# Ten HBM tiles for first weight sums, and normalisation of q, k and spatial v in four parts

## The chip, the cores and the metric

One core of a Trainium2 chip runs the whole layer in one launch. The metric is the device time of one execution in microseconds. Five engines work side by side, each through its own queue of instructions: TensorE (PE; PEld are its weight loads), VectorE (DVE), ScalarE (ACT), GpSimd (POOL) and SyncE (SP), which here only issues DMA transfers. An engine waits for another through semaphores.

## What is computed

The reference is one decoder layer on 256 tokens of width 2048 in float32. An RMS norm of x is followed by one wide projection into nine parts: q, k, v and z_a for attention, u_b, v_b and z_b for spatial gating, and two gates g_a and g_b.

```python
h = rms_norm(x, norm_g)
q, k, v, z_a, u_b, v_b, z_b, g_a, g_b = jnp.split(h @ w_in, cuts, axis=-1)
q = rms_norm(q.reshape(B, S, 8, 128), q_norm_g)
k = rms_norm(k.reshape(B, S, 8, 128), k_norm_g)
y_a = (moba_attention(q, k, v) * jax.nn.silu(z_a)) @ w_proj_a
sgu = spatial_gating(gelu(u_b), gelu(v_b), sgu_norm_g, w_s, b_s)
y_b = (sgu * jax.nn.silu(z_b)) @ w_proj_b
return x + (sigmoid(g_a) * y_a + sigmoid(g_b) * y_b) @ w_out
```

With 256 tokens the attention is causal inside one block. spatial_gating normalises v_b per group of 128 columns (an RMS norm with a gain), mixes positions with a causal 128x128 matrix per group, and multiplies by u_b. So q, k and v_b are each normalised per head or group: a sum of squares over 128 columns, the inverse root, and a scaling.

## The kernel before, in words

**Work and its tiles.** Weights stream from HBM in 120 granules of 128 x 2048 floats (1 MB), each laid out by the host as four 128 x 512 blocks. The list `G` of `schedule()` has the order: 8 granules each for q (0 to 7), k (8 to 15), v (16 to 23), za (24 to 31), vb (32 to 39), ub (40 to 47) and zb (48 to 55); then four times 8 granules of a gate quad (the gates' columns) and 4 of a projection (56 to 103); then two out quads (104 to 119).

**Precision.** Every float32 product is made of three matmuls: a weight block is split into a high part `wh`, rounded to the type float32r, and a rest `wl`, and so is x; TensorE adds high times high, low times high and high times low (`three`, line 318, whose matmul is line 323). `split` (line 152) makes the parts: a cast on ScalarE (line 149 or 171) and a subtraction on VectorE (line 150 or 176).

**Sum granules.** Some granules of each quad after q are multiplied by a scheme with seven block products in place of eight (`strassen(i)` says which; `seven`, line 341). They also need three sums of weight blocks, `t` (VectorE, lines 172 to 174), split in turn into `th` (ScalarE, line 175) and `tl` (VectorE, line 177). Five of the eight granules of k, v, vb and zb are of this kind, four of za and ub, five of the first gate quad, six of the other three. There is one buffer for `t`, three each for `wh`, `wl` and `th`, two for `tl`, and four for `raw`, the loaded weights.

**The first weight sum, made in HBM.** The first of these sums (block 12 plus block 11) isn't made by an engine: `pre_copy` (line 127) has SyncE copy block 12 into a tile of the HBM ring, `pre_sum` (line 132) has GpSimd start a DMA that adds block 11 to it, and `load` (line 136) later loads that tile as the first block of `raw`, followed by the remaining 768 KB. The ring has six tiles (line 113). In iteration i of the main loop the load of granule i + 3 is issued, then the copy for i + 8 and the accumulation for i + 6, then the split of i + 2, and then granule i's matmuls.

```python
            load(i + 3)
        if i >= 1:
            pre_copy(i + 8)
            pre_sum(i + 6)
        split(i + 2, 2 if i < 2 else 1)
```

**Work between the granules.** The dictionary `later` says what is called behind the matmuls of a granule. `sums` (line 394) makes 16 sums of squares on ScalarE (line 401), four for each of the four 128 x 512 tiles of q, k or v_b, and per tile the inverse root: a small VectorE operation into `ms` (line 268), a power on GpSimd into `rs` (line 269) and, for k, a VectorE multiplication (line 406). `norm_qk` (line 409) and `norm_v` (line 417) scale with 16 ScalarE operations (lines 415 and 423); `norm_v` also multiplies by the gain on VectorE. For q the sums are called behind granule 9 and the scaling behind 11; for k behind 17 and 19; for v_b behind 42 and 44. Their consumers are the transposes `turn_qk` behind granules 16 (q) and 24 (k) and `mix` behind 48. `softmax` has two calls behind granule 26, and its results are transposed behind 32.

**What sets the order.** SyncE and GpSimd execute in the order in which the program is written, in the whole kernel (line 109). ScalarE and VectorE do so only for the first eight granules (line 658). From granule 8 on, their order and TensorE's come from a planner that runs when the program is built: it prefers instructions that stand earlier in the program, but lets a later one go first when it thinks that the earlier one isn't ready. Once planned, each engine's order is fixed.

Of the kernel before, what the change touches and what calls it, by code (L numbers as in the profile page):

```python
# [12 lines left out]
F32 = mybir.dt.float32  # L13
# [3 lines left out]
AF = mybir.ActivationFunctionType  # L17
ALU = mybir.AluOpType
AX = mybir.AxisListType

P = 128
# [8 lines left out]
B = 512  # L30
# [41 lines left out]
def hybrid_layer_kernel(  # L72
# [9 lines left out]
    nc = tc.nc  # L82
# [7 lines left out]
    small = ctx.enter_context(tc.tile_pool(name="small", bufs=4))  # L90
    psum = ctx.enter_context(tc.tile_pool(name="psum", bufs=1, space=bass.MemoryType.PSUM))
    dram = ctx.enter_context(tc.tile_pool(name="dram", bufs=1, space=bass.MemoryType.DRAM))
# [4 lines left out]
    def u(name, dtype=F32):  # L97
        return unit.tile([P, B], dtype, tag="u", name=name)
# [11 lines left out]

    raw, wh, wl, th, tl = {}, {}, {}, {}, {}
    pre = {}
    ring = [dram.tile([P, B], F32, tag=f"ring{n}", name=f"ring{n}") for n in range(6)]

    def strassen(i):
        if i >= NG or G[i][0] != "quad" or G[i][1] == G[0][1]:
# [10 lines left out]
    def pre_copy(i):  # L127
        if i < NG and strassen(i):
            pre[i] = ring[len(pre) % len(ring)]
            nc.sync.dma_start(pre[i], w[i, :, 0:B])  # L130

    def pre_sum(i):
        if i in pre:
            nc.gpsimd.dma_start(pre[i], w[i, :, B:2 * B], accum_op=ALU.add)  # L134
# [44 lines left out]
    X = {}  # L179

    def heads(ap):
        return ap.rearrange("p (h d) -> p h d", d=P)
# [65 lines left out]
    gain = const.tile([P, P], F32, name="gain")  # L248
# [17 lines left out]
    def rsqrt(dst, src, n, count):  # L266
        ms = small.tile([P, 8], F32, tag="ms", name="ms")
        nc.vector.tensor_scalar(ms[:, :n], src, 1.0 / count, EPS, op0=ALU.mult, op1=ALU.add)
        nc.gpsimd.tensor_tensor(dst, ms[:, :n], mhalf[:, :n], op=ALU.pow)
# [121 lines left out]
        return [[c11, c12], [h, c22]]  # L391


    def sums(C, name):
        for m in range(2):
            for c in range(2):
                ss = small.tile([P, 4], F32, tag="ss", bufs=8, name="ss")
                junk = u("junk")
                scale = rstd[:, m:m + 1] if name == "k" else 1.0
                for h in range(4):  # L400
                    nc.scalar.activation(junk[:, h * P:(h + 1) * P], C[m][c][:, h * P:(h + 1) * P], AF.Square,
                                         scale=scale, accum_out=ss[:, h:h + 1])
                rs = small.tile([P, 4], F32, tag="rs", bufs=8, name="rs")
                rsqrt(rs, ss, 4, P)
                if name == "k":
                    nc.vector.tensor_scalar(rs, rs, scale, None, op0=ALU.mult)
                X["rs", name, m, c] = rs

    def norm_qk(name):
        C = X[name]  # L410
        for m in range(2):
            for c in range(2):
                for h in range(4):
                    sl = C[m][c][:, h * P:(h + 1) * P]
                    nc.scalar.activation(sl, sl, AF.Copy, scale=X["rs", name, m, c][:, h:h + 1])

    def norm_v():
        C = X["vb"]
        for m in range(2):
            for c in range(2):  # L420
                for h in range(4):
                    sl = C[m][c][:, h * P:(h + 1) * P]
                    nc.scalar.activation(sl, sl, AF.Copy, scale=X["rs", "vb", m, c][:, h:h + 1])
                t = heads(C[m][c])
                nc.vector.tensor_tensor(t, t, gain[:, None, :].to_broadcast([P, 4, P]), op=ALU.mult)

    def func(name, fn):
        for m in range(2):
# [168 lines left out]
    def at(i, fn, *a):  # L597
        later.setdefault(i, []).append((fn, a))
# [14 lines left out]
    at(i0 + 6, halves_f, "x")  # L613
    at(i0 + 8, halves_4)
    i0 = first["k", 0]
    at(i0 + 1, sums, None, "q")
    at(i0 + 3, norm_qk, "q")
    i0 = first["v", 0]
    at(i0 + 0, turn_qk, "q", None)
    at(i0 + 1, sums, None, "k")  # L620
    at(i0 + 3, norm_qk, "k")
    i0 = first["za", 0]
    at(i0 + 0, turn_qk, "k", None)
    at(i0 + 1, score, None)
    at(i0 + 2, softmax, 0)
    at(i0 + 2, softmax, 1)
    i0 = first["vb", 0]
    at(i0 + 0, turn_p, 0, None)
    at(i0 + 0, turn_p, 1, None)
# [5 lines left out]
    at(i0 + 0, turn_z, "za", None)  # L635
    at(i0 + 0, causal_mix)
    at(i0 + 1, func, "vb", AF.Gelu_apprx_tanh)
    at(i0 + 2, sums, None, "vb")
    at(i0 + 4, norm_v)
    i0 = first["zb", 0]  # L640
    at(i0 + 0, mix, None)
    at(i0 + 1, func, "ub", AF.Gelu_apprx_tanh)
# [37 lines left out]
    for i, (kind, name, c, kp, n) in enumerate(G):  # L680
        if i == 8:
            ordered.close()
        if i:
            load(i + 3)
        if i >= 1:
            pre_copy(i + 8)
            pre_sum(i + 6)
        split(i + 2, 2 if i < 2 else 1)
        if i < 4:
            split_x(i + 4)  # L690
# [44 lines left out]
                merge(c, Y)  # L735
        for fn, a in later.pop(i, []):
            a = list(a)
            if fn is sums:
                a[0] = X[a[1]]
            elif a and fn in (turn_qk, score, turn_p, attend, turn_z, mix, turn_m):  # L740
                if a[-1] is None:
                    a[-1] = list(E)
                    if fn is turn_p and a[0] == 1:
                        a[-1] = [E[3], E[0], E[1]]
                    if fn is attend:
                        a[-1] = E[2 * a[0]:]
                elif a[-1] == "late":
                    a[-1] = E[2:4] + L[0:2]
                elif a[-1] == "L01":
                    a[-1] = L[0:2]  # L750
                elif a[-1] == "L23":
                    a[-1] = L[2:4]
                elif a[-1] == "L3":
                    a[-1] = L[3:4]
            fn(*a)
# [48 lines left out]
```

## Time and profile before

| what | value |
|---|---|
| median of three runs | 670.8 us (667.85 to 671.66) |
| the profiled execution | 668.79 us, its span 667.1 us |
| TensorE busy | 653.7 us, 2959 matmuls |
| VectorE busy | 601.8 us, 587 instructions |
| ScalarE busy | 432.3 us, 521 instructions |
| GpSimd busy | 73.2 us, 85 instructions |
| bytes moved by DMA | 166.28 MB, mean 249 GB/s |

All rows but the first come from one profiled execution; the span runs from its first instruction to its last. A row of a timeline has the start in microseconds from the start of the span, the duration, the engine, the line of the kernel, the operation, what is written <- what is read, and the count of operations merged into the row. In brackets stands the idle time of the engine before it, with what ended that. A row of the waits has the waiting engine, tile and line, after the arrow whom it waited for, then the microseconds in total, how often, and the longest. A row of a group has the count, the busy time in microseconds, the mean of one in nanoseconds and the idle time before, with its reasons. An engine name with a small q (SPq) is the queue that issues DMA transfers.

### The profile page before, as it was taken

The page shows a single profiled execution, that of the slowest core. Times are in us where ns is not written, and L with a number is a line of the kernel's source. Part 1 is how long each engine was busy: PE and PEld are TensorE (multiplying, and loading weights), DVE is VectorE, ACT ScalarE, POOL GpSimd, SP SyncE. Part 2 cuts the span into 40 slices and gives each one's busy share as a digit, 9 for nine tenths or more (in the row PEclk, how much of TensorE's full clock was granted, in tenths as well). Part 3 has the DMA queues.
Part 4 walks back from the last instruction along what each step waited for, and adds up shares of the span by engine and source line. Part 5 has one row for each costly group of instructions (what it writes and reads, how often), then busy time and mean ns, then how long its engine had stood idle before and what let it go on. Part 6 is the DMA issues. An engine that isn't in the chain of part 4 may idle for free.

```text
span 667.1 us, 8042 instructions
## 1 busy us (share of the span) xinstructions
PE 653.7 (98%) x2959; PEld 533.4 (80%) x2959; DVE 601.8 (90%) x587; ACT 432.3 (65%) x521; POOL 73.2 (11%) x85
## 2 busy tenths in 40 slices
PE   8999899999999999999999999999999999999997
PEld 4888678788888788888877887788788878888875
DVE  4779888999898999999998999979988998999896
ACT  7968949857877679685654755556555564754360
POOL 1110503101000305000001100100010000000000
PEclk9999989999999999999999999999999999999999
DMA  8998894789687858967658973995598599777841
GB/s 303 396 407 272 257 333 145 208 282 271 176 284 219 257 201 251 329 194 235 220 205 271 283 250 145 340 289 199 194 350 249 204 276 307 242 181 246 235 200 63
DMA packets 47703, 166.28 MB, mean 249 GB/s; under 512 B 5296, under 2 KB 5936, under 8 KB 40112
## 3 DMA queue, kind: packets, MB, share of 16 engines
q1 hardware_dynamic: 38016, 148.21, 60.2%
q0 software_dynamic: 8496, 15.47, 15.6%
q10 hardware_dynamic: 1152, 2.10, 1.0%
q8 instruction: 23, 0.38, 0.2%
q14 instruction: 16, 0.13, 0.0%
HBM read 163.66 MB, written 33.03 MB: 295 GB/s over the span
## 4 chain that ended last, share of the span: by engine, by line
PE 67%; DVE 13%; ACT 8%; DMA 6%; issue 4%; POOL 1%; SPq 0%; DVEq 0%; ACTq 0%; POOLq 0%
PE y L323 13%; PE acc_g L323 11%; PE seven_g L323 6%; DMA raw<-in_w 6%; PE acc_za L323 5%; PE acc_ub L323 4%; PE acc_zb L323 4%; PE acc_vb L323 4%; DVE wl L176 3%; ACT wh L149 3%; PE acc_out L323 3%; DVE wl L150 3%; DVE tl L177 3%; PE acc_v L323 2%; PE seven_zb L323 2%
## 5 line engine op out<-in xcount | busy, mean ns | idle before, releaser
L150 DVE TENSOR_TENSOR wl<-raw,wh 128x2048 fp32r<-128x2048 f32 (+2 forms) x69 | 140.2, 2039 | 21.3 <-ACT wh L149 21.3
L149 ACT CAST wh<-raw 128x2048 fp32r<-128x2048 f32 (+2 forms) x69 | 117.4, 1713 | 60.5 <-PE acc_g L323 19.5
L171 ACT CAST wh<-raw 128x2048 fp32r<-128x2048 f32 x59 | 112.6, 1914 | 61.5 <-issue 12.8
L176 DVE TENSOR_TENSOR wl<-raw,wh 128x2048 fp32r<-128x2048 f32 x59 | 134.8, 2286 | 6.6 <-ACT wh L171 6.4
L175 ACT CAST th<-t 128x1536 fp32r<-128x1536 f32 x59 | 87.5, 1483 | 59.5 <-DVE t L174 58.1
L177 DVE TENSOR_TENSOR tl<-t,th 128x1536 fp32r<-128x1536 f32 x59 | 103.9, 1760 | 5.2 <-ACT th L175 5.2
L134 POOL DMA_DIRECT2D ring<-in_w x59 | 49.0, 882 | 456.0 <-DMA ring<-in_w 438.4
L172 DVE TENSOR_TENSOR t<-raw 128x512 f32<-128x512 f32 x59 | 40.9, 693 | 10.0 <-DMA raw<-in_w 9.4
L173 DVE TENSOR_TENSOR t<-t,raw 128x512 f32<-128x512 f32 x59 | 40.6, 687 | 0.9
L174 DVE TENSOR_TENSOR t<-t,raw 128x512 f32<-128x512 f32 x59 | 40.4, 684 | 0.0
L323 PE MATMUL acc_g<-wh,xul 128*128 128x512 f32 x99 | 38.6, 390 | 0.0
L323 PE MATMUL acc_g<-wl,xuh 128*128 128x512 f32 x99 | 38.6, 389 | 0.0
L323 PE MATMUL acc_g<-wh,xuh 128*128 128x512 f32 x99 | 38.5, 389 | 0.0
L323 PE MATMUL acc_out<-wl,mh 128*128 128x512 f32 x72 | 28.2, 391 | 0.8 <-DVE wl L150 0.8
L323 PE MATMUL acc_out<-wh,mh 128*128 128x512 f32 x72 | 28.0, 390 | 0.0
L323 PE MATMUL acc_out<-wh,ml 128*128 128x512 f32 x72 | 28.0, 391 | 0.0
L323 PE MATMUL acc_q<-wh,xuh 128*128 128x512 f32 x64 | 25.1, 392 | 1.7 <-ACT wh L149 1.7
L323 PE MATMUL acc_q<-wl,xuh 128*128 128x512 f32 x64 | 25.3, 396 | 0.4 <-DVE wl L150 0.2
L323 PE MATMUL y<-wh,zbl 128*128 128x512 f32 x64 | 25.1, 392 | 0.0
L323 PE MATMUL y<-wh,zal 128*128 128x512 f32 x64 | 25.0, 390 | 0.0
L323 PE MATMUL acc_q<-wh,xul 128*128 128x512 f32 x64 | 25.0, 390 | 0.0
L323 PE MATMUL y<-wl,zah 128*128 128x512 f32 x64 | 24.9, 389 | 0.0
(542 smaller groups left out, 1586.7 us busy)
## 6 DMA issues: line engine op xcount, KB each, us to landing
raw<-in_w SPq DMA_DIRECT2D x57, 1024.0 KB, 7.3
raw<-in_w SPq DMA_DIRECT2D x59, 768.0 KB, 6.7
ring<-in_w SPq DMA_DIRECT2D x59, 256.0 KB, 7.9
ring<-in_w POOLq DMA_DIRECT2D x59, 256.0 KB, 7.6
raw<-ring SPq DMA_DIRECT2D x59, 256.0 KB, 4.6
raw<-in_w SPq DMA_DIRECT2D x7, 512.0 KB, 8.7
xnat<-in_x SPq DMA_DIRECT2D x2, 1024.0 KB, 15.5
xres<-in_x ACTq DMA_DIRECT2D x8, 256.0 KB, 3.7
```

The lines of the kernel that those rows point to most:

```text
L134: nc.gpsimd.dma_start(pre[i], w[i, :, B:2 * B], accum_op=ALU.add)
L149: nc.scalar.copy(h, r)
L150: nc.vector.tensor_tensor(l, r, f(h), op=ALU.subtract)
L171: nc.scalar.copy(wh[i], r)
L172: nc.vector.tensor_tensor(T2, r[:, 0:B], r[:, 2 * B:3 * B], op=ALU.add)
L173: nc.vector.tensor_tensor(T1, T2, r[:, B:2 * B], op=ALU.subtract)
L174: nc.vector.tensor_tensor(T3, T2, r[:, 3 * B:], op=ALU.add)
L175: nc.scalar.copy(th[i], t)
L176: nc.vector.tensor_tensor(wl[i], r, f(wh[i]), op=ALU.subtract)
L177: nc.vector.tensor_tensor(tl[i], t, f(th[i]), op=ALU.subtract)
L323: nc.tensor.matmul(acc, a, b, start=(start and n == 0), stop=(stop and n == 2))
```

## The change

The HBM ring gets ten tiles. For granules up to 15 copies and accumulations stay eight and six iterations ahead; from granule 16 on they are eleven and eight ahead. `sums` and the two scaling functions are rewritten to handle one of four tiles per call. The four calls of `sums` stand behind four successive granules: 9 to 12 for q, 17 to 20 for k, 42 to 45 for v_b. The four of `norm` begin two granules later: 11 to 14, 19 to 22 and 44 to 47. The order of the four tiles becomes (0, 0), (1, 0), (0, 1), (1, 1). The second call of `softmax` moves from granule 26 to 27.

```diff
--- before.py
+++ after.py
@@ -110,7 +110,7 @@
 
     raw, wh, wl, th, tl = {}, {}, {}, {}, {}
     pre = {}
-    ring = [dram.tile([P, B], F32, tag=f"ring{n}", name=f"ring{n}") for n in range(6)]
+    ring = [dram.tile([P, B], F32, tag=f"ring{n}", name=f"ring{n}") for n in range(10)]
 
     def strassen(i):
         if i >= NG or G[i][0] != "quad" or G[i][1] == G[0][1]:
@@ -391,38 +391,32 @@
         return [[c11, c12], [h, c22]]
 
 
-    def sums(C, name):
-        for m in range(2):
-            for c in range(2):
-                ss = small.tile([P, 4], F32, tag="ss", bufs=8, name="ss")
-                junk = u("junk")
-                scale = rstd[:, m:m + 1] if name == "k" else 1.0
-                for h in range(4):
-                    nc.scalar.activation(junk[:, h * P:(h + 1) * P], C[m][c][:, h * P:(h + 1) * P], AF.Square,
-                                         scale=scale, accum_out=ss[:, h:h + 1])
-                rs = small.tile([P, 4], F32, tag="rs", bufs=8, name="rs")
-                rsqrt(rs, ss, 4, P)
-                if name == "k":
-                    nc.vector.tensor_scalar(rs, rs, scale, None, op0=ALU.mult)
-                X["rs", name, m, c] = rs
-
-    def norm_qk(name):
-        C = X[name]
-        for m in range(2):
-            for c in range(2):
-                for h in range(4):
-                    sl = C[m][c][:, h * P:(h + 1) * P]
-                    nc.scalar.activation(sl, sl, AF.Copy, scale=X["rs", name, m, c][:, h:h + 1])
-
-    def norm_v():
-        C = X["vb"]
-        for m in range(2):
-            for c in range(2):
-                for h in range(4):
-                    sl = C[m][c][:, h * P:(h + 1) * P]
-                    nc.scalar.activation(sl, sl, AF.Copy, scale=X["rs", "vb", m, c][:, h:h + 1])
-                t = heads(C[m][c])
-                nc.vector.tensor_tensor(t, t, gain[:, None, :].to_broadcast([P, 4, P]), op=ALU.mult)
+    QUARTERS = ((0, 0), (1, 0), (0, 1), (1, 1))
+
+    def sums(name, n):
+        m, c = QUARTERS[n]
+        C = X[name][m][c]
+        ss = small.tile([P, 4], F32, tag="ss", bufs=8, name="ss")
+        junk = u("junk")
+        scale = rstd[:, m:m + 1] if name == "k" else 1.0
+        for h in range(4):
+            nc.scalar.activation(junk[:, h * P:(h + 1) * P], C[:, h * P:(h + 1) * P], AF.Square,
+                                 scale=scale, accum_out=ss[:, h:h + 1])
+        rs = small.tile([P, 4], F32, tag="rs", bufs=8, name="rs")
+        rsqrt(rs, ss, 4, P)
+        if name == "k":
+            nc.vector.tensor_scalar(rs, rs, scale, None, op0=ALU.mult)
+        X["rs", name, n] = rs
+
+    def norm(name, n):
+        m, c = QUARTERS[n]
+        C = X[name][m][c]
+        for h in range(4):
+            sl = C[:, h * P:(h + 1) * P]
+            nc.scalar.activation(sl, sl, AF.Copy, scale=X["rs", name, n][:, h:h + 1])
+        if name == "vb":
+            t = heads(C)
+            nc.vector.tensor_tensor(t, t, gain[:, None, :].to_broadcast([P, 4, P]), op=ALU.mult)
 
     def func(name, fn):
         for m in range(2):
@@ -613,17 +607,19 @@
     at(i0 + 6, halves_f, "x")
     at(i0 + 8, halves_4)
     i0 = first["k", 0]
-    at(i0 + 1, sums, None, "q")
-    at(i0 + 3, norm_qk, "q")
+    for n in range(4):
+        at(i0 + 1 + n, sums, "q", n)
+        at(i0 + 3 + n, norm, "q", n)
     i0 = first["v", 0]
     at(i0 + 0, turn_qk, "q", None)
-    at(i0 + 1, sums, None, "k")
-    at(i0 + 3, norm_qk, "k")
+    for n in range(4):
+        at(i0 + 1 + n, sums, "k", n)
+        at(i0 + 3 + n, norm, "k", n)
     i0 = first["za", 0]
     at(i0 + 0, turn_qk, "k", None)
     at(i0 + 1, score, None)
     at(i0 + 2, softmax, 0)
-    at(i0 + 2, softmax, 1)
+    at(i0 + 3, softmax, 1)
     i0 = first["vb", 0]
     at(i0 + 0, turn_p, 0, None)
     at(i0 + 0, turn_p, 1, None)
@@ -635,8 +631,9 @@
     at(i0 + 0, turn_z, "za", None)
     at(i0 + 0, causal_mix)
     at(i0 + 1, func, "vb", AF.Gelu_apprx_tanh)
-    at(i0 + 2, sums, None, "vb")
-    at(i0 + 4, norm_v)
+    for n in range(4):
+        at(i0 + 2 + n, sums, "vb", n)
+        at(i0 + 4 + n, norm, "vb", n)
     i0 = first["zb", 0]
     at(i0 + 0, mix, None)
     at(i0 + 1, func, "ub", AF.Gelu_apprx_tanh)
@@ -682,9 +679,11 @@
             ordered.close()
         if i:
             load(i + 3)
-        if i >= 1:
-            pre_copy(i + 8)
-            pre_sum(i + 6)
+        for j in range(i + 6, i + 12):
+            if j == i + (8 if j < 16 else 11):
+                pre_copy(j)
+            if j == i + (6 if j < 16 else 8):
+                pre_sum(j)
         split(i + 2, 2 if i < 2 else 1)
         if i < 4:
             split_x(i + 4)
@@ -735,9 +734,7 @@
                 merge(c, Y)
         for fn, a in later.pop(i, []):
             a = list(a)
-            if fn is sums:
-                a[0] = X[a[1]]
-            elif a and fn in (turn_qk, score, turn_p, attend, turn_z, mix, turn_m):
+            if a and fn in (turn_qk, score, turn_p, attend, turn_z, mix, turn_m):
                 if a[-1] is None:
                     a[-1] = list(E)
                     if fn is turn_p and a[0] == 1:
```

## The prediction, made before the result was known

> **What bounds the kernel now.** I read the page's busy shares first, then TensorE's stalls (the view of waits, then the timeline where one was long), then the sums by stage, and last the timelines of the engines that came late.
>
> ```profile
> span 667.1 us, 8042 instructions
> ## 1 busy us (share of the span) xinstructions
> PE 653.7 (98%) x2959; PEld 533.4 (80%) x2959; DVE 601.8 (90%) x587; ACT 432.3 (65%) x521; POOL 73.2 (11%) x85
> ```
>
> TensorE is busy 98% of the span. Nothing in the change takes a matmul away, so it can only win what TensorE loses: places where it stood still or ran slower than its usual pitch. The longest such place after the start lies in granule 13, one of the k quad's:
>
> ```profile
> 79.50 0.39 PE L323 MATMUL seven_k<-wl,Fhx 128*128 128x512 f32 x1
> ...
> 83.18 0.50 PE L323 MATMUL seven_k<-tl,Fhx 128*128 128x512 f32 x1 [1.89 <-DVE tl L177]
> ...
> 83.74 0.63 PE L323 MATMUL seven_k<-th,Fhx 128*128 128x512 f32 x1
> ...
> 87.15 0.39 PE L323 MATMUL acc_k<-wh,xul 128*128 128x512 f32 x1
> 87.38 0.39 PE L323 MATMUL acc_k<-wh,xuh 128*128 128x512 f32 x1
> ```
>
> The first column is the start. The usual pitch is the 0.23 us between the last two rows. From 79.50 to 87.15 the timeline has 13 steps; at 0.2275 us each they need 2.96 us and took 7.65, so 4.7 us are lost here. Two things make that up. TensorE waits, first for th and then 1.89 us for tl: about 3.1 us. Then, between 83.74 and 87.15, eight matmuls take 3.41 us, 0.43 each instead of 0.23: another 1.6 us at about half speed. The sums by stage show it in the clock column (the last but two), 0.91 against 1.00 in the stretch from 40 to 60:
>
> ```profile
> 40.00:60.00 20.00, 20.00 (x90) 16.57 (x89) 17.04 (x16) 16.95 (x17) 3.27 (x4) 1.00 1.03 354
> ...
> 80.00:100.00 20.00, 17.56 (x68) 13.77 (x69) 18.06 (x17) 10.54 (x12) 1.64 (x2) 0.91 1.00 330
> ```
>
> The columns are: stretch, its length, busy time of PE, PEld, DVE, ACT and POOL, clock, DMA share, GB/s. I take the slow stretch to be a consequence of the stall, since it follows at once and nothing is waited for in it. By the Trainium skill ("TensorE: Matmul & The Clock Gate", Part 1, the HAM clock gate) the clock halves after an idle window of about 3.4 us; by that rule this stall, well under 3.4 us, would not have cost the 1.6 us, and removing it would bring that much less, 666.6 us instead of the forecast below. The measured pitch decides here: it did slow down.
>
> Why th and tl of granule 13 were late is seen on ScalarE (first five rows) and VectorE (the rest):
>
> ```profile
> 63.44 0.34 ACT L401 ACTIVATE junk<-q 128x128 f32<-128x128 f32 x1
> ...
> 67.54 1.91 ACT L171 CAST wh<-raw 128x2048 fp32r<-128x2048 f32 x1
> ...
> 72.53 4.80 ACT L415 ACTIVATE q<-q,rs 128x128 f32<-128x128 f32 x16
> 77.22 1.91 ACT L171 CAST wh<-raw 128x2048 fp32r<-128x2048 f32 x1
> 79.01 1.49 ACT L175 CAST th<-t 128x1536 fp32r<-128x1536 f32 x1
> ```
>
> ```profile
> 69.48 2.29 DVE L176 TENSOR_TENSOR wl<-raw,wh 128x2048 fp32r<-128x2048 f32 x1 [1.17 <-ACT wh L171]
> ...
> 76.89 0.69 DVE L174 TENSOR_TENSOR t<-t,raw 128x512 f32<-128x512 f32 x1
> 79.16 2.29 DVE L176 TENSOR_TENSOR wl<-raw,wh 128x2048 fp32r<-128x2048 f32 x1 [1.59 <-ACT wh L171]
> 81.37 1.75 DVE L177 TENSOR_TENSOR tl<-t,th 128x1536 fp32r<-128x1536 f32 x1
> ```
>
> ScalarE spends 63.44 to 67.54 on fourteen of q's sixteen square sums and 72.53 to 77.3 on all sixteen scalings, both in one piece. Behind each block stands a cast wh, and VectorE, which needs it for wl, idles 1.17 and 1.59 us. VectorE has t of granule 13 ready at 77.58; th starts at 79.01, behind the cast of granule 14; tl ends at 83.12, and TensorE resumes at 83.18.
>
> The second place is the four gate quads.
>
> ```profile
> PE seven_g L323 <- ACT th L175: 0.9, 1, 0.9
> ```
>
> The weight loads of the three later gate quads wait for tl in the view of waits, and VectorE, in the whole span, for loads:
>
> ```profile
> PEld seven_g L323 <- DVE tl L177: 3.1, 6, 1.0
> ```
>
> ```profile
> DVE t L172 <- DMA raw<-in_w: 9.4, 3, 4.2
> ```
>
> The longest of VectorE's three waits, in its timeline, with the issue of the load it waits for, in SyncE's, and the median landing time of such loads from the page's DMA issues:
>
> ```profile
> 440.44 0.69 DVE L172 TENSOR_TENSOR t<-raw 128x512 f32<-128x512 f32 x1 [4.24 <-DMA raw<-in_w]
> ```
>
> ```profile
> 426.91 0.43 SPq L122 DMA_DIRECT2D raw<-in_w  x1
> ```
>
> ```profile
> raw<-in_w SPq DMA_DIRECT2D x59, 768.0 KB, 6.7
> ```
>
> And the sums by stage for that stretch and for the third gate quad:
>
> ```profile
> 420.00:440.00 20.00, 20.00 (x89) 16.18 (x88) 14.76 (x15) 10.10 (x9) 3.28 (x4) 1.00 1.04 340
> 451.80:492.40 40.60, 39.98 (x176) 32.33 (x175) 39.08 (x32) 22.71 (x14) 2.47 (x3) 1.00 0.64 223
> ```
>
> In the quad VectorE is busy 39.08 of 40.60 us: it can only just feed TensorE. It enters each of these quads late, because it stood waiting for the first sum granule's weights, 4.24 us before 440.44. That transfer left at 426.91 and took over 13 us where the median is 6.7, in a stage (projection granules) in which the DMA engines were full (1.04). There the copies and accumulations of six sums fall together with the loads.
>
> **The change, part by part.** It removes and adds no instruction: square sums, rsqrt, scalings and HBM copies keep their number and shapes. All terms are moves.
>
> *Sums and scalings of q and k in four parts.* Each part of four squares or four scalings is about 1.2 us on ScalarE (4.80 / 4), and in program order a part now stands behind the next granule's split, so the planner, which prefers earlier work, can let the cast wh go ahead of three of the four parts. If both VectorE waits go, tl of granule 13 ends 2.76 us earlier, at 80.36. TensorE would want it at 79.50 + 3 x 0.2275 = 80.18. A stall of 0.2 us is left, too short for the slow stretch, and 4.5 us are won. If only the first wait goes (1.17), tl ends at 81.95, and some 1.2 to 2.8 us are won. If the planner, finding ScalarE free and all parts ready, lines them up as before, nothing is won. TensorE's earlier arrival then meets the v quad:
>
> ```profile
> 97.50:140.30 42.80, 42.35 (x191) 34.04 (x191) 39.58 (x42) 35.58 (x66) 8.23 (x8) 1.00 0.66 203
> ```
>
> ```profile
> PE acc_v L323 <- DVE wl L176: 0.3, 1, 0.3
> ```
>
> ```profile
> DVE rs L406 <- POOL rs L269: 3.1, 4, 1.1
> ```
>
> ```profile
> L269 POOL TENSOR_TENSOR rs<-ms,mhalf 128x4 f32<-128x4 f32 x12 | 16.9, 1414 | 58.7 <-DVE ms L268 58.7
> ```
>
> VectorE is busy 39.58 of 42.80 us in v, and 3.1 of the 3.2 it is idle are waits for GpSimd's power, which k's sums need four times. So v has almost no slack to swallow an earlier TensorE, and I let it take back 1 us. The bounds for q and k together are -2.5 us (a loss; the rival on GpSimd below) and +5.0 (the 4.7 and v's own wait of 0.3). I take **3.5 us**, nearer the upper end because the two waits that the block causes are in the rows.
>
> *Spatial v in four parts.* No stall of TensorE in ub is due to these blocks; four scalings and one multiply by the gain simply run one to three granules later, and their consumer, the mix at zb's first granule, comes one granule after the last part. I cost it at 0. If that cover is gone, the mix's PSUM banks come free late and the first zb sum waits for them; a slip of one part is 1.2 us. *softmax 1* comes one granule later, five ahead of its transposes: 0.
>
> *Copies eleven and accumulations eight ahead.* For sums from granule 16 on SyncE issues the copy three iterations earlier, past three loads, and GpSimd the accumulation two earlier. Ten HBM tiles hold all sums between copy and load (at most eight granules), so the copy waits for no tile. On GpSimd the accumulations now stand ahead of the powers of the same iteration, behind copies that were issued three iterations before: no new wait. A granule of a gate quad takes 5 us (40.60 / 8), so the copies for the next gate quad leave some 15 us earlier. They then fall mostly in the gate quad before, whose DMA share is about 0.64, and most accumulations, which follow their copies, are done before the projection loads. With the median 6.7 us the load of 426.91 would land at 433.6, before VectorE asks for it at 436.2 (440.44 - 4.24), and the wait would be gone. Of the six weight-load waits of 3.1 us, a load that runs under the matmul before it hides up to one pitch each, so 1.7 (3.1 - 6 x 0.23) to 3.1 us are lost; the 9.4 us that VectorE can get back is more than that. I take 1.9. In the first gate quad a cast that waits for its load holds th back:
>
> ```profile
> 360.02 1.91 ACT L149 CAST wh<-raw 128x2048 fp32r<-128x2048 f32 x1 [3.58 <-DMA raw<-in_w]
> 361.83 1.47 ACT L175 CAST th<-t 128x1536 fp32r<-128x1536 f32 x1
> ```
>
> This is the 0.9 us stall of seven_g for th. About one copy fewer (256 KB, 0.7 us at 340 GB/s) runs beside that load, so I add 0.4. Together **2.3 us**, bounds -1.5 and 4.0 (3.1 + 0.9). The lower end stands for the other side of the move: the v quad's first two copies now leave some three granules earlier, in the stretch from 40 to 60 us, where the DMA engines are full as well (1.03, above). Two copies of 256 KB are 1.5 us at 354 GB/s. In the two engines' timelines no split of the k quad waits for a load, so I expect no cost.
>
> **The sum.** 3.5 + 2.3 = 5.8 us. The profiled execution took 668.8 us (667.1 of span and 1.7 around it), so it becomes 663.0. It lies 2.0 us below the median of the runs, 670.8; on the median the forecast is **665.0 us**. The start (granules 0 to 7), the out quads and their waits are untouched.
>
> **Rivals.** *VectorE takes it back* (0.12). The k stall goes, but v and the quads after it are paced by VectorE, and TensorE waits there instead. For it: 39.58 of 42.80 us busy in v. Against it: VectorE's own idle time, 2.76 us in k, is removed by the same edit. Then the gate gain is left: 668.5 us. *The order stays* (0.12). The planner still packs the parts into ScalarE's first free gap, because they are ready; the stall at 79.5 stays whole. For it: priority only decides between ready instructions. Against it: squares of parts 1 to 3 now rank behind a cast that is ready. Again 668.5 us. *GpSimd's trips pace VectorE* (0.14), the slower case. Its place is k's sums in v. Today four powers overlap partly and VectorE waits 3.1 us; spread over four granules each trip can stand alone, 4 x 1.41 = 5.6 us, 2.5 us more on an engine with 0.1 us to spare. If the k stall stays as well and the new wait falls in one place, the slow stretch of 1.6 us is paid a second time: 670.8 + 4.1 = 674.9 us. It decides as soon as the four waits exceed 3.1 us by more than the other moves win.
>
> **How the numbers follow.** A measurement of this kernel can tell about 0.5%, 3.4 us, from no change. The forecast case (0.62) is faster by more than that and has its own range, 661.8 (both upper bounds, 9.0 us) to 667.4; the first two rivals (0.24) are within it, the third (0.14) above. The range 661 to 672.5 takes in the forecast, both equal cases and the near part of the slower one; left out are the far part of the third rival and gains past the upper bounds by more than 0.8 us of spread between runs.
>
> **What would show it.** Right: the squares and scalings of q appear on ScalarE in groups of four with casts between; no wait of seven_k over 1 us near 80 us and no 0.43 us pitch behind it; VectorE's waits for raw in the projection stages fall well below 9.4 us, and the DMA share there falls below 1. Wrong: seven_k still waits for tl, the four waits of VectorE for rs sum to over 5 us, or the gate quads keep their waits for tl although the loads come earlier.

## The result and the profile after

The kernel after takes 672.65 us (median of 17 runs, 671.42 to 676.48); the kernel before, run beside it, 667.49 (17 runs, 665.78 to 671.66). The ratio is 1.0071, 95% interval 1.0055 to 1.0087: slower by 0.7%, where faster was forecast, and 0.15 us above the top of the range. The profiled execution took 672.78 us, of which the span is 671.0; that of before took 668.79.

The page after, its first lines:

```profile
span 671.0 us, 8030 instructions
...
PE 654.4 (98%) x2959; PEld 533.1 (79%) x2959; DVE 601.5 (90%) x587; ACT 432.1 (64%) x521; POOL 74.3 (11%) x85
```

Busy times hardly move, as was said; only where TensorE stands still has changed. The starts of the quads in TensorE's timeline tell where. The planner lets a few matmuls of the next quad go early, so a quad's start is counted here: it is the start of the matmul that stands behind as many weight matmuls as the quads before it have (us; the last column is a kernel of the experiments):

| stretch | before | after | copies alone |
|---|---|---|---|
| k quad (granules 8 to 15) | 45.09 | 50.56 | 42.32 |
| v quad (16 to 23) | 43.49 | 44.92 | 43.50 |
| za, vb, ub, zb (24 to 55) | 183.63 | 183.66 | 183.16 |
| gate quads, projections, out quads to the span's end | 343.1 | 340.1 | 341.4 |

Each column is one execution. A second one of the copies alone reads 44.06, 43.49, 183.15 and 339.67, so a k quad is read to some 1.7 us only, and so is the last row. In the copies alone granule 8 starts at 53.0 and 52.8 us, in the other two at 51.8.

So the two halves of the change part ways. From the gate quads on 3.0 us are won, in the places that were named. In k and v 6.9 us are lost, where 3.5 were to be won. The sums by stage show it too; of before the second stretch was shown, and the first is

```profile
60.00:80.00 20.00, 19.89 (x88) 16.00 (x86) 17.21 (x18) 20.00 (x55) 8.85 (x7) 1.00 0.77 246
```

After:

```profile
60.00:80.00 20.00, 16.41 (x70) 12.63 (x70) 15.74 (x15) 15.93 (x45) 7.67 (x5) 1.00 0.90 293
80.00:100.00 20.00, 16.86 (x63) 12.52 (x63) 17.08 (x15) 13.34 (x18) 5.02 (x5) 0.91 0.78 229
```

Before, from 60 to 80, ScalarE was full and TensorE nearly. After, TensorE is busy only 16.41 of 20 us, VectorE 15.74 and ScalarE 15.93: nobody is full, so somebody waits for a chain. ScalarE's timeline after, in the k quad:

```profile
67.92 0.30 ACT L403 ACTIVATE junk<-q 128x128 f32<-128x128 f32 x1
...
72.38 1.28 ACT L416 ACTIVATE q<-q,rs 128x128 f32<-128x128 f32 x4 [4.07 <-POOL rs L269]
...
73.86 1.89 ACT L171 CAST wh<-raw 128x2048 fp32r<-128x2048 f32 x1
75.66 1.46 ACT L175 CAST th<-t 128x1536 fp32r<-128x1536 f32 x1
```

The scalings do stand in groups of four, and the squares in groups of one to four, with casts between. But the first scaling of q stands right behind the squares, and ScalarE waits 4.07 us in front of it for rs, with the casts wh and th queued behind. What rs waited for, in GpSimd's and in VectorE's timeline:

```profile
67.53 4.82 POOL L269 TENSOR_TENSOR rs<-ms,mhalf 128x4 f32<-128x4 f32 x1 [15.94 <-DVE ms L268]
```

```profile
67.28 0.17 DVE L268 TENSOR_SCALAR ms<-ss 128x4 f32<-128x4 f32 x1
67.35 0.68 DVE L172 TENSOR_TENSOR t<-raw 128x512 f32<-128x512 f32 x1
67.95 2.28 DVE L176 TENSOR_TENSOR wl<-raw,wh 128x2048 fp32r<-128x2048 f32 x1
...
70.76 0.68 DVE L174 TENSOR_TENSOR t<-t,raw 128x512 f32<-128x512 f32 x1
71.36 0.17 DVE L268 TENSOR_SCALAR ms<-ss 128x4 f32<-128x4 f32 x1
75.79 2.29 DVE L176 TENSOR_TENSOR wl<-raw,wh 128x2048 fp32r<-128x2048 f32 x1 [4.26 <-ACT wh L171]
```

A power on 512 numbers took 4.82 us; it ran as long as VectorE streamed (67.35 to 71.44) and ended shortly after VectorE stopped. VectorE then idled 4.26 us for the cast that ScalarE held back. The cast is granule 13's; tl of granule 12 stands behind it in VectorE's order. TensorE pays twice in a row, for granule 12 (first four rows) and then for granule 13 (last row):

```profile
77.17 0.50 PE L323 MATMUL seven_k<-th,Flx 128*128 128x512 f32 x1 [0.87 <-ACT th L175]
...
79.80 0.50 PE L323 MATMUL seven_k<-tl,Fhx 128*128 128x512 f32 x1 [1.90 <-DVE tl L177]
...
81.04 0.63 PE L323 MATMUL acc_k<-th,xul 128*128 128x512 f32 x1
81.47 0.63 PE L323 MATMUL acc_k<-th,xuh 128*128 128x512 f32 x1
...
88.52 0.50 PE L323 MATMUL seven_k<-tl,Fhx 128*128 128x512 f32 x1 [1.89 <-DVE tl L177]
```

Granule 12's stall is new. The pitch behind it, from 81.04 to 81.47, is 0.43 us, as behind the stall of before. Granule 13's is the stall of before, still 1.89 us; this time no slow stretch follows it. All who waited for a rs, in the answer for that tile:

```profile
  ACT q L416: 5.1, 2
  ACT vb_c L416: 3.8, 1
  DVE rs L408: 3.3, 3
```

The columns are who waited, us in total and how often. Before, only the last group was there, at 3.1 us. VectorE's waits for loads in the whole span, and the weight loads' waits for tl in the three later gate quads, show the other half of the change:

```profile
DVE t L172 <- DMA raw<-in_w: 7.1, 3, 3.6
```

```profile
PEld seven_g L323 <- DVE tl L177: 2.1, 6, 0.7
```

9.4 us became 7.1, and 3.1 became 2.1. The DMA share hardly fell: in the 20 us that answer to 420 to 440 of before (425.3 to 445.3, as TensorE comes 5.3 us later) it is 0.99, where it was 1.04.

### The profile page after: what moved, and what is told of

Same layout as the page of the kernel before. It is cut to its first block, busy times and chain, and to the rows that moved or that the text cites. A ratio compares the mean times of both kernels' runs of the same rounds, so it can differ in the third digit from the quotient of the medians.

```text
span 671.0 us, 8030 instructions
## 1 busy us (share of the span) xinstructions
PE 654.4 (98%) x2959; PEld 533.1 (79%) x2959; DVE 601.5 (90%) x587; ACT 432.1 (64%) x521; POOL 74.3 (11%) x85
## 4 chain that ended last, share of the span: by engine, by line
PE 68%; DVE 10%; issue 10%; DMA 5%; ACT 5%; POOL 2%; SPq 0%; DVEq 0%; ACTq 0%; POOLq 0%
PE acc_g L323 14%; PE y L323 13%; PE seven_g L323 9%; DMA raw<-in_w 5%; PE acc_ub L323 4%; PE acc_za L323 4%; PE acc_vb L323 4%; PE acc_zb L323 3%; PE acc_out L323 3%; DVE wl L150 3%; ACT wh L149 2%; DVE wl L176 2%; PE seven_vb L323 2%; DVE tl L177 2%; PE seven_ub L323 2%
## 5 line engine op out<-in xcount | busy, mean ns | idle before, releaser
L134 POOL DMA_DIRECT2D ring<-in_w x59 | 50.7, 901 | 408.8 <-DMA ring<-in_w 408.8
L269 POOL TENSOR_TENSOR rs<-ms,mhalf 128x4 f32<-128x4 f32 x12 | 21.8, 1820 | 88.4 <-DVE ms L268 88.4
```

## The experiments

The theory after the first look ("the trip"): a part's sum goes from ScalarE over VectorE (mean square) to GpSimd (power) and back, and takes up to 5 us; whole, sixteen scalings came about 5 us behind the last square and found all rs made; cut, the planner puts a scaling right behind a sum, and the wait stands on ScalarE in front of casts. Rivals: the copies ahead hurt the k quad; the new orders of ScalarE and TensorE cost by themselves; only VectorE's stops for rs of k matter. Medians are each beside the kernel before on the same chip.

### The two halves apart

Copies alone (before, with the new copies and accumulations), and parts alone (after, with the old ones):

```diff
-    ring = [dram.tile(...) for n in range(6)]
+    ring = [dram.tile(...) for n in range(10)]
...
-        if i >= 1:
-            pre_copy(i + 8)
-            pre_sum(i + 6)
+        for j in range(i + 6, i + 12):
+            if j == i + (8 if j < 16 else 11):
+                pre_copy(j)
+            if j == i + (6 if j < 16 else 8):
+                pre_sum(j)
```

> Kernel before with ten HBM tiles and the copies and accumulations further ahead; sums and scalings as before. Trip theory (the loss of the change comes from ScalarE standing at a scaling of q whose rs GpSimd hasn't delivered): the k quad (start of granule 8 to start of 16) takes about 45 us as in before, the gate quads win the 2 to 3 us seen between the two traces, 664 to 665 us in all. Rival (the earlier copies crowd the loads of the k quad and cost the time): k quad about 50 us and 671 us or more in all.

Measured: 665.42 us, ratio 0.9969 [0.9953, 0.9986]; 0.4 us over the theory's range and far under the rival's. On another chip, with more runs:

> The copies and accumulations ahead with ten tiles alone once more, on the chip of these runs and with more rounds: 664.5 to 666.5 us, 0.2 to 0.45% under the kernel before; the yardstick for the kernel with the sums on GpSimd.

Measured: 665.81 us, ratio 0.9969 [0.9951, 0.9986]. The two profiled executions of this one kernel put granule 16 at 95.35 and at 96.89 us.

> The changed kernel with six HBM tiles and the old distances of copies and accumulations; only the four parts and the moved softmax call remain. Trip theory: k quad about 50 us with ScalarE waiting 4 us or more for rs, v quad 1 to 2 us longer than before, 673 to 675 us. Rival (copies): about 668 us.

Measured: 675.7 us, ratio 1.0124 [1.0094, 1.0154], the median of four runs; 0.7 us over the theory's range. The k quad takes 49.6 us, and the v quad, at 47.0, loses more than the 1 to 2 us expected. ScalarE's timeline of the parts alone has the same two waits for rs of q as after, the second of 1.02 us, the first here:

```profile
71.41 1.28 ACT L416 ACTIVATE q<-q,rs 128x128 f32<-128x128 f32 x4 [4.05 <-POOL rs L269]
```

The copies win 2.0 and 1.8 us, the parts lose 8.3 without them; beside them the loss is 1.0071 - 0.9969 = 1.0%, some 6.8 us. The copies ahead are acquitted.

### Which part

q in one piece again, k and spatial v in parts:

```diff
-    for n in range(4):
-        at(i0 + 1 + n, sums, "q", n)
-        at(i0 + 3 + n, norm, "q", n)
+    for n in (0, 2, 1, 3):
+        at(i0 + 1, sums, "q", n)
+        at(i0 + 3, norm, "q", n)
```

> The changed kernel with q's sums and scalings again in one piece each (behind granules 9 and 11); k and spatial v stay in four parts, copies stay ahead. Trip theory: k quad back to about 45 us, no wait of ScalarE for q's rs, v quad still 1 to 2 us longer than before; 666 to 667 us. If the loss sat in the parts of k or spatial v instead, it stays above 670.

Measured: 670.62 us, ratio 1.0061 [1.0041, 1.0081]: a miss, over the 666 to 667 us of the theory and in the range that was named for a loss in the parts of k or spatial v. The k quad came down to 46.5 us, but the v quad rose to 48.6. TensorE stands still in it at four places, for 4.8 us in all. The first three (0.8, 1.0 and 0.6 us) lie behind these waits, in VectorE's timeline:

```profile
111.77 0.23 DVE L408 TENSOR_SCALAR rs<-rs,rstd 128x4 f32<-128x4 f32 x1 [0.33 <-POOL rs L269]
113.68 0.23 DVE L408 TENSOR_SCALAR rs<-rs,rstd 128x4 f32<-128x4 f32 x1 [1.67 <-POOL rs L269]
113.82 0.16 DVE L268 TENSOR_SCALAR ms<-ss 128x4 f32<-128x4 f32 x1
115.64 0.23 DVE L408 TENSOR_SCALAR rs<-rs,rstd 128x4 f32<-128x4 f32 x1 [1.66 <-POOL rs L269]
```

For k VectorE itself stands in the trip, since it multiplies rs by rstd, and it took the third mean square only behind the second product: 3.7 us in a row, with all subtractions behind it, and a fourth wait of 0.90 later; 4.6 us in all, against 3.1 before. This is the slower rival of the prediction, at the place it named. The fourth and longest place has another cause, as TensorE's and ScalarE's timelines show:

```profile
143.04 0.50 PE L323 MATMUL seven_v<-th,xul 128*128 128x512 f32 x1 [2.33 <-ACT th L175]
```

```profile
139.71 1.91 ACT L149 CAST wh<-raw 128x2048 fp32r<-128x2048 f32 x1 [3.15 <-DMA raw<-in_w]
```

There a weight load came late. The profiled execution took 673.62 us, 3.0 over the median of this kernel, so this profile doesn't say how much of the v quad's 5.1 us k's parts cost in a usual run. The other way round, k in one piece and q and spatial v in parts (the same edit on k's loop):

> The kernel after, with the sums and scalings of k in one piece at their old places; q and spatial v stay in four parts. Theory (the loss of the k quad is q's parts, that of the v quad is k's parts): k quad as in the kernel after, 49.5 to 51 us, v quad 43.3 to 44.3 us (after 44.9, copies alone 43.5), time 670.5 to 672.5 us. Rival (the v quad is late because of what q's parts left behind it): v quad 44.7 us or more, time 672.5 to 674 us.

Measured: 670.46 us, ratio 1.0048 [1.0032, 1.0063]; k quad 50.2 us, v quad 43.0 (0.3 under the theory's range), and ScalarE's two waits for rs of q sum to 5.1 us, as after.

So q's parts cost the k quad and k's parts the v quad. The losses don't add up: over the ratio of the copies alone, 0.9% are lost with q whole, 0.8% with k whole and 1.0% with both cut, and with both cut the v quad loses only 1.4 us. That TensorE arrives late in it may be the reason; no run shows it.

### The trip taken away

After, with rs of q, k and spatial v made on VectorE as a reciprocal of the mean square (another scale than the layer's):

```diff
-        nc.gpsimd.tensor_tensor(dst, ms[:, :n], mhalf[:, :n], op=ALU.pow)
+        if n == 4:
+            nc.vector.reciprocal(dst, ms[:, :n])
+        else:
+            nc.gpsimd.tensor_tensor(dst, ms[:, :n], mhalf[:, :n], op=ALU.pow)
```

> The changed kernel, but rs of q, k and spatial v is made by VectorE as a reciprocal of the mean square instead of by GpSimd as its power -0.5 (so q, k and spatial v are scaled by another number). ScalarE's order in the k quad is the same as in the changed kernel, only the trip to GpSimd is gone. Trip theory: ScalarE no longer waits before the first scaling of q, the cast behind it starts some 4 us earlier, k quad 45 to 46 us, 665 to 667 us. Rival (the order of the parts among the casts costs the time by itself): k quad stays near 50 us, 671 us or more.

Measured: 665.06 us, ratio 0.9964 [0.9947, 0.9981]. The matmuls stand in the same order as after, yet nothing stops in front of the first scaling:

```profile
67.71 1.28 ACT L419 ACTIVATE q<-q,rs 128x128 f32<-128x128 f32 x4
69.17 1.90 ACT L171 CAST wh<-raw 128x2048 fp32r<-128x2048 f32 x1
```

The whole loss of the parts is gone with the trip; TensorE's new order is innocent. But nothing is won over the copies alone either. That left open whether cutting is worth the forecast 3.5 us once the trip is gone: the same reciprocals with sums and scalings whole, beside this kernel again.

> The copies alone, with rs of q, k and spatial v made on VectorE as the reciprocal of the mean square in place of the power -0.5 on GpSimd (so the scale is another one than the layer's): sums and scalings whole, no trip. Beside it the kernel with four parts and the same reciprocals. Theory (without the trip the parts are worth what the prediction said): 3 us or more slower than the four parts, 668 us or more. Rival (the cast that leaves the sixteen scalings' block only stands behind another one, and cutting wins nothing even without the trip): within 1.5 us of the four parts, 663.5 to 666.5 us; then no wait of VectorE for rs, the v quad at 41.7 to 42.5 us, and seven_k's wait for tl at 1.5 us or more in both.

> The kernel after with the reciprocals on VectorE once more, beside the whole sums and scalings with the same reciprocals: 664 to 666 us; the yardstick for that kernel.

Measured: whole 664.5 us, ratio 0.9943 [0.9929, 0.9956]; in parts 665.5 us, ratio 0.9957 [0.9943, 0.997]. The rival holds for the time: cutting wins nothing even without the trip. Of the whole kernel no profile near its median was kept, so what it was to show of waits and the v quad stays unread. In parts, without the trip, TensorE still has the old wait, at 82.82 in the first profile where the kernel before had it at 83.18, and at 82.24 (1.88 us) in the second. In the first:

```profile
82.82 0.50 PE L326 MATMUL seven_k<-tl,Fhx 128*128 128x512 f32 x1 [1.89 <-DVE tl L177]
```

What stands in front of it, in ScalarE's and in VectorE's timeline of that profile, is granule 14's cast and the subtraction that waits for it:

```profile
76.88 1.90 ACT L171 CAST wh<-raw 128x2048 fp32r<-128x2048 f32 x1
```

```profile
78.81 2.29 DVE L176 TENSOR_TENSOR wl<-raw,wh 128x2048 fp32r<-128x2048 f32 x1 [1.56 <-ACT wh L171]
```

Before, this cast started at 77.22 and this wait was 1.59 us. Of q's sixteen scalings the plan has eleven, and all the squares, ahead of the cast. So of the two waits of VectorE that were to go, cutting took away the first, the 1.17 us in front of granule 12's subtraction, and not the second.

### Sums whole, or scalings later

After with all four sums at the first place and the scalings in parts (`at(i0 + 1, sums, "q", n)`, the same for k, and `i0 + 2` for spatial v):

> The kernel after, with all four square sums of q, of k and of spatial v called at the first place again, so that only the scalings are in four parts; the copies and accumulations stay ahead. Theory (a trip of a sum over VectorE and GpSimd and back is too long for a scaling that stands right behind the next part's squares in ScalarE's order): the squares go first again and the scalings find their rs made, so no scaling of q waits for GpSimd (under 0.5 us in all, after: 5.1), k quad 43 to 45 us from its first granule to v's (after 50.6), time 664 to 667.5 us. Rival (the order that TensorE and ScalarE get from cut scalings costs by itself): TensorE's order here is that of the kernel after, so k quad stays at 48 us or more and the time at 670 us or more.

Measured: 668.23 us, ratio 1.0009 [0.9992, 1.0026]; 0.7 us over the theory's range, and under the rival's. No scaling waits for rs: all mean squares are made before the next cast is there to be subtracted, VectorE has three narrow operations and then idles 1.18 us, and four powers together take 6.32 us, in GpSimd's timeline:

```profile
66.34 6.32 POOL L269 TENSOR_TENSOR rs<-ms,mhalf 128x4 f32<-128x4 f32 x4 [15.92 <-DVE ms L268]
```

The k quad is at 44.4 us. The v quad keeps 45.2: the cut scalings of k make VectorE take two subtractions in a row ahead of tl, which costs TensorE waits of 0.6, 1.0 and 0.5 us. After with each scaling of q and k called two granules later (`at(i0 + 5 + n, norm, ...)` for `i0 + 3 + n`):

> The kernel after, with each scaling of q and of k called two granules later (four granules behind its sum, not two); the cuts, the distances of spatial v and the copies stay. Theory (only the distance between a sum and its scaling is too short): ScalarE's waits for rs of q fall from 5.1 us to under 1.5, the k quad from 50.6 to 44 to 46.5 us, and the time to 665 to 668.5 us. Rival (VectorE's and GpSimd's order is what loses the time, wherever the scaling stands): k quad 49 us or more, time 671 us or more.

Measured: 668.84 us, ratio 1.0014 [0.9998, 1.003]; k quad 45.3 us, time 0.3 us above the range. The first power is as slow as ever, and is now covered:

```profile
66.11 4.82 POOL L269 TENSOR_TENSOR rs<-ms,mhalf 128x4 f32<-128x4 f32 x1 [15.92 <-DVE ms L268]
```

```profile
75.81 1.28 ACT L416 ACTIVATE q<-q,rs 128x128 f32<-128x128 f32 x4 [1.03 <-POOL rs L269]
```

Of the 5.1 us that ScalarE waited for rs of q this 1.03 is left. Distance alone takes 5.2 of the k quad's 5.5 lost us back (50.56 to 45.34), and leaves the v quad's (45.0). Against the copies alone (0.9969) both kernels of this section still lose 0.4%.

### Without VectorE in the trip

Mean square, power and k's product all on GpSimd, once with the copies alone and once with the parts:

```diff
-        nc.vector.tensor_scalar(ms[:, :n], src, 1.0 / count, EPS, op0=ALU.mult, op1=ALU.add)
+        nc.gpsimd.tensor_scalar(ms[:, :n], src, 1.0 / count, EPS, op0=ALU.mult, op1=ALU.add)
...
-                    nc.vector.tensor_scalar(rs, rs, scale, None, op0=ALU.mult)
+                    nc.gpsimd.tensor_scalar(rs, rs, scale, None, op0=ALU.mult)
```

> The copies alone (first weight sums further ahead, sums and scalings whole), with the mean square, the power and k's product with rstd all on GpSimd, so that VectorE issues nothing of them. Theory (VectorE stops in its order for each trip of k): VectorE's waits for rs, 2.8 us in the copies alone, go; VectorE comes to the v quad's subtractions earlier and the v quad falls from 43.5 to 42.5 to 43.2 us; ScalarE waits for no rs, since the whole scalings still come a block later; 663.8 to 665.2 us, a little under the copies alone. Rival (GpSimd's three small instructions for each part are held by VectorE's streams, and the scalings wait): ScalarE waits over 1 us for rs, 666 us or more.

Measured: 665.22 us, ratio 0.9962 [0.9946, 0.9978], beside 0.9969 of the copies alone: the v quad fell to 41.9 us, further than the theory's 42.5 to 43.2, while the k quad reads 46.4, and the time can't be told apart. No version that computes the layer beats the copies alone by what a measurement here can tell. The whole sums with the reciprocals read lower, 0.9943, but they scale by another number, and were not run beside the copies alone.

> The kernel after, with the mean square, the power and k's product on GpSimd: VectorE has no part in the trips, ScalarE's order in the k quad stays. Theory (in the k quad the loss is ScalarE's wait at the first scalings of q, not VectorE's place in the trip): ScalarE still waits 4 us or more for rs of q, k quad 49 to 51.5 us, v quad 43.3 to 45 us, time 670 to 673 us. Rival (what loses the time is VectorE, which takes the mean squares late and stops for rs): k quad 46.5 us or less, time under 668 us.

Measured: 671.07 us, ratio 1.0028 [1.0001, 1.0054]; k quad 47.8 us, v quad 45.8. Neither theory comes out whole: the time is that of the first, the k quad lies between. The v quad is 0.8 us over the first theory's range. The planner's order moved with the edit, and the waits with it: ScalarE waited 2.6 us for rs of k, 2.3 for spatial v's and 1.6 for q's, and nobody else waited for a rs. The edit also made GpSimd's share of the trip longer: its products of k took 0.3 to 3.0 us. So taking VectorE out in this way doesn't cure the parts; what VectorE's share alone costs, it doesn't tell.

### The power by itself

> Not the layer: this kernel leaves all of its computation out. GpSimd raises 128x4 numbers to the power -0.5 in 24 powers, four of each kind: with VectorE idle, and beside trains of VectorE: one subtraction of two 128x2048 tiles, four of them, eight additions of two 128x512 tiles, four scalings of one 128x2048 tile, and eight additions of a bank of PSUM and a 128x512 tile. Theory (VectorE's streams from two SBUF tiles hold a power until they pause): 1.0 to 1.6 us alone, 2.3 to 2.9 beside one subtraction, 4.5 us or more beside four of them and beside eight narrow additions, 1.0 to 1.6 beside scalings of one tile and beside the bank. Rival (the long powers are GpSimd's own, from its queue of transfers): 1.0 to 1.6 us in all kinds.

One execution. GpSimd's timeline, one power of each kind and both kinds of the narrow additions:

```profile
6.43 1.01 POOL L110 TENSOR_TENSOR rs_none<-ms_none,mhalf 128x4 f32<-128x4 f32 x1 [5.60 <-DVE ms_none L109]
...
11.61 2.98 POOL L110 TENSOR_TENSOR rs_wide<-ms_wide,mhalf 128x4 f32<-128x4 f32 x1 [0.28 <-DVE ms_wide L109]
...
24.65 2.98 POOL L110 TENSOR_TENSOR rs_widex<-ms_widex,mhalf 128x4 f32<-128x4 f32 x1 [0.28 <-DVE ms_widex L109]
...
61.83 1.43 POOL L110 TENSOR_TENSOR rs_narrow<-ms_narrow,mhalf 128x4 f32<-128x4 f32 x1 [6.27 <-DVE ms_narrow L109]
66.77 5.59 POOL L110 TENSOR_TENSOR rs_narrow<-ms_narrow,mhalf 128x4 f32<-128x4 f32 x1 [3.51 <-DVE ms_narrow L109]
...
88.40 2.41 POOL L110 TENSOR_TENSOR rs_single<-ms_single,mhalf 128x4 f32<-128x4 f32 x1 [2.64 <-DVE ms_single L109]
...
108.44 1.01 POOL L110 TENSOR_TENSOR rs_bank<-ms_bank,mhalf 128x4 f32<-128x4 f32 x1 [3.90 <-DVE ms_bank L109]
```

VectorE's trains beside the second, third and fifth of these:

```profile
11.44 2.28 DVE L120 TENSOR_TENSOR wl<-raw,wh 128x2048 f32<-128x2048 f32 x1
...
24.48 9.27 DVE L120 TENSOR_TENSOR wl<-raw,wh 128x2048 f32<-128x2048 f32 x4
...
66.60 4.90 DVE L127 TENSOR_TENSOR wl<-raw,wh 128x512 f32<-128x512 f32 x8
```

Alone a power takes 1.01 us; beside a train that reads a bank of PSUM and one tile of SBUF, also 1.01. Beside trains of two SBUF tiles it is held: until the end of the subtraction that had begun (11.44 + 2.28 = 13.72, power over at 14.59), or, twice in four times, to the end of all eight narrow additions (66.60 + 4.90 = 71.50, over at 72.36); the other two slipped in at 1.4. Beside four subtractions it got its turn after the first, so that 4.5 us or more, which was expected there, did not come; and scalings of one tile, expected to leave it alone, held it to 2.4. The rival is out: no transfer is queued on GpSimd in this kernel.

## Why the prediction was wrong

**The step that failed** is "Sums and scalings of q and k in four parts": taken as 3.5 us won, it cost some 6.8. Its sentence that "the planner, which prefers earlier work, can let the cast wh go ahead of three of the four parts" went astray in two ways. The planner did mix parts and casts, but it put the first scaling ahead of granule 13's cast, where rs was not there: ScalarE waited 4.07 us, and VectorE 4.26 for the cast, which it had not done before. And granule 14's cast, the one behind the 1.59 that was to be removed, went ahead of the last part of the scalings only; that wait became 2.69. Only the first of the two waits, 1.17, went. The prediction knew the price of a power only as a mean, 1.41 us, and asked who waits for rs only on VectorE, in v. That ScalarE's scalings wait for rs as well, and had found it ready only because they came a block later, wasn't asked.

**The two waits of VectorE as the cause of the stall.** This was not put to the test, because the second wait never went. Without the trip it is 1.56 and 1.58 us in two profiles, tl of granule 13 ends at 82.77 and 82.18, where 81.95 was worked out for the first wait alone, and TensorE's wait for it is 1.89 and 1.88. That is why, as far as the timelines tell, cutting wins nothing even without the trip: VectorE has a subtraction wl and then tl to do, 2.3 and 1.75 us, from the time ScalarE gives it the next cast, while TensorE wants tl one matmul behind th. Whether the stall would go if the second wait did, no run shows.

**The slow stretch of 1.6 us** was counted as part of the stall. It is not a fixed part: it comes and goes between executions of one kernel (last section).

**The -2.5 as lower bound** was too near. It came from GpSimd's trips on VectorE; the kind was right, and in the kernel with q whole it stood just where the rival said (waits of 4.6 us, against 5.6 worked out), though not spread out but three in a row; but the dearer place was ScalarE, and a power can take more than three times its mean.

**v takes 1 us back.** The v quad is 1.43 us longer, but for another reason than TensorE's early arrival: it arrived 5.5 us late.

**Spatial v at 0.** vb's first scalings wait 3.8 us for rs. Little of it reaches TensorE: ub's and zb's sixteen granules together took 86.97 us, against 86.52 before and 86.51 with the copies alone, so 0.45 us. In the two profiles of the parts without the trip they took 87.7, with a wait of zb's for tl of 0.9 us, so the parts of spatial v may cost something by themselves.

**Copies and accumulations ahead, 2.3 us.** Right in kind, and nearly in size: 2.0 and 1.8 us alone. The 0.9 us stall of the first gate quad is gone, as said. VectorE's wait for the load that came 4.24 us late fell to 2.37 and did not vanish; the next, 3.78 us, fell only to 3.62. In the two profiles of the copies alone these two are 2.58 and 4.32, and 2.48 and 2.66. And in the first of them one stall of 0.94 us for tl is left in the last gate quad.

**The sum.** In the profiled executions: 5.5 + 1.4 + 0.0 - 3.0 = 3.9 us, the spans' 667.1 to 671.0. The base was off too: three runs had a median of 670.8, seventeen have 667.49. That the copies alone come out at 665.4 and 665.8, next to the 665.0 forecast for the whole change, is chance. The list of what would show it wrong held: seven_k still waited for tl. Its second item, four waits of VectorE over 5 us, would have missed the cause: they are 3.3.

## What to carry to other kernels

Before cutting a block into parts, follow each part's input round: when a value goes over another engine and back, the distance between asking and using is what counts, and a whole block may have hidden a trip that a part can't. Price the trip at its longest case beside the other engines' work, not at its mean. And look in the planned order whether the work that waits behind the block really went ahead of the parts: here the cast moved by less than a microsecond even where the parts cost nothing, and nothing was won.

## What the runs showed of the hardware

A power of 128x4 takes 1.01 us alone and up to 5.59 beside VectorE's operations on two SBUF tiles (4.82 in the layer); beside operations with one operand in PSUM it stays at 1.01. For two SBUF tiles this agrees with the Trainium skill ("GPSIMD Engine Reference", 1. Specifications), by which GpSimd shares its SBUF interfaces with VectorE and contends with instructions that have two SBUF inputs or run in a 2-port mode. Whether the scalings of one tile, which held a power to 2.41 us, ran in such a mode, no run here shows. The runs add that a single small operation can be held through several of VectorE's.

The half-speed stretch came after idle times of TensorE under the 3.1 us of before, and not always. Two kernels with a stall at the same place of the k quad, in TensorE's timeline; first the copies alone in their second run:

```profile
83.16 0.50 PE L323 MATMUL seven_k<-tl,Fhx 128*128 128x512 f32 x1 [1.83 <-DVE tl L177]
...
84.68 0.63 PE L323 MATMUL acc_k<-th,xuh 128*128 128x512 f32 x1
85.11 0.63 PE L323 MATMUL acc_k<-tl,xuh 128*128 128x512 f32 x1
```

and the kernel with the scalings two granules later:

```profile
82.94 0.50 PE L323 MATMUL seven_k<-tl,Fhx 128*128 128x512 f32 x1 [1.89 <-DVE tl L177]
...
84.20 0.39 PE L323 MATMUL acc_k<-th,xuh 128*128 128x512 f32 x1
84.43 0.39 PE L323 MATMUL acc_k<-tl,xuh 128*128 128x512 f32 x1
```

After 1.83 us the pitch was 0.43, after 1.89 it was 0.23. Two executions of one kernel, the parts with the reciprocals, part in the same way: 0.43 after 1.89 us, 0.23 after 1.88. So the length of the stall doesn't settle alone whether the 1.6 us follow; what does stays open.
